# A residual block on one core: the first units' weights loaded from the middle of the output projection, and two accumulators exchanged in its second half

## The chip, the core and the metric

The kernel runs on one core of a Trainium2 chip. Its time is the device time of one execution in microseconds (us). Several executions are timed and their median is given; one more is taken with the hardware profiler, and all rows quoted below are of that one.

## What is computed

One layer on x of 512 tokens by 2048 features, all float32: a normalisation, an input projection, eight heads each of two kinds of attention, an output projection with a residual, a normalisation and a feed-forward part with 8192 hidden features.

```python
h = rmsnorm(x, g_attn);  proj = h @ w_in                  # 2048 x 6152
mixed = concat(headnorm(stick_breaking(qa, ka, va)), headnorm(forgetting(qf, kf, vf, log_f)))
x = x + mixed @ w_out                                     # 2048 x 2048: around the change
u = relu(rmsnorm(x, g_mlp) @ w_up)                        # 2048 x 8192
x = x + (u * u) @ w_down                                  # 8192 x 2048
y = rmsnorm(x, g_final)
```

## The kernel before, in words

**Numbers in two parts.** Every float32 operand is split into a high part (a rounding that ScalarE makes, a CAST of L63) and a low part (what is left, a subtraction of VectorE, L64). A product is three matmuls: high by high, high by low, low by high (L96 to L98, function mm3). ScalarE is called ACT below, VectorE DVE, TensorE PE, and SP is the engine that issues nearly all transfers. The parts of weights go into pairs of tiles named wh and wl, of which three pairs take turns.

**Seven products for eight.** The output projection, and both feed-forward matrices, are multiplied block by block in a scheme with seven products, numbered 1 to 7, of sums and differences of the four blocks of each operand. Some of the sums of w_out are made during the attention and put into DRAM (wsums, whigh). The left operand's seven forms for the output projection are G; for the feed-forward part they are F, made by left_form from hr, the new x after transposing.

**The output projection** (L682 to L762) runs through two halves of columns, db = 0 and 1, and in each through the products in the order G_ORDER = 1, 2, 6, 5, 7, 3, 4. A product has four pieces (function out_piece, m0 = 4, 6, 0, 2). For each piece SP loads a raw tile of 512 KB (wo, L630 from w_out or L632 from wsums; three raw buffers take turns), the piece is split into wh and wl, and PE runs 12 matmuls of 512 columns. Products 5 and 6 of the first half load ready high and low parts instead (L611 and L612, with wx tiles of a pool px as an additional buffer).

**The accumulators.** PSUM has three tiles A, B, C of two banks each (accoa, accob, accoc in the profile). Products 1, 6, 7 and 4 sum into A, 2 into B, 5 and 3 into C. Product 6 continues on what 1 left in A, 7 on 6, 4 on 7; 3 continues on 5. After each product take (L647) has DVE add the accumulator to a quarter of x (L651). After products 2, 7, 3 and 4 a quarter is finished: turn_quarter has PE transpose it (tr, L662), ACT copy it into hr (L665), and SP store it (xd, L666). begin (L645) loads a quarter's x ahead.

**What comes after it.** The feed-forward part's first matrix is worked off in units of 256 hidden features. A unit loads its weights in two transfers of 1 MB (L534, tiles wu of a pool rw), makes seven forms of them with DVE (L540 to L546), and runs its products in accumulators psa, psb, psc (pool ups), which stand in the same six banks as A, B and C. Later units load their weights when they are made; units 0 and 1 are loaded during the output projection. The first unit's product 1 starts when the output projection's product 4 of the second half is over.

**Who sets the order.** Each engine runs its own instructions in order. That order is written when the kernel is built: instructions go by the order of the program text, and by when their inputs and buffers come free in a simulation. issue_after(i) puts an instruction behind another on the same engine; in the loop it holds a unit's load behind the last weight transfer of the product after which it stands. A tile of a pool that takes over another pool's place waits for that tile's last reader.

**The places that the change touches** are the loop's end of a product:

```python
if db == 0 and p == 3:                      # L722: mixed is given up, rw takes its place
    mixp_cm.__exit__(None, None, None)
    rw = ctx.enter_context(tc.tile_pool(name="rw", bufs=5, side="right", reuse_waits="tile"))
if db == 1 and p in (2, 5, 7, 3):           # L725: a half of unit 0 or 1
    u, k = divmod((2, 5, 7, 3).index(p), 2)
    with tc.issue_after(ins.ins):           # ins: the product's last weight transfer
        if k == 0:
            units.append(Unit(u))
        units[u].load(k)
if db == 0 and p == 5:                      # L732: px is given up
    more_parts.pop()
    px_cm.__exit__(None, None, None)
```

and out_piece's choice of accumulator (L617), take (L647), and Unit.multiply (L554), where the first unit's three accumulators are given banks in the order c, a, b.

## Time and profile before

| what | value |
|---|---|
| median of 3 runs | 2080.78 us (2080.08 to 2081.69) |
| the profiled execution | 2079.1 us, a span of 2077.4 us |
| granted TensorE clock | 0.999 |
| busy | PE 99%, weight loads 88%, DVE 78%, ACT 51%, POOL 3% |
| moved by transfers | 394.20 MB, 190 GB/s on average |

The span is the time from the program's first instruction to its last; the execution's own time is 1.7 us longer. In a row of a timeline stand the start in us from the beginning of the span, the time taken, the engine, the line, the operation, the tile written and the tile read, and in brackets how long the engine had been idle and what ended that. A row for SP is an issue; "x4" means that four such instructions were merged, and the time is that from the first to the last one's end. A row "DMA wo<-..." is a transfer from its issue to its landing. The stretch around the output projection goes from about 630 to 810 us: its first half to 719, its second half from 720 to 804.

### The profile page before, as it was taken

The page shows a single profiled execution, that of the slowest core. Times are in us where ns is not written, and L with a number is a line of the kernel's source. Part 1 is how long each engine was busy: PE and PEld are TensorE (multiplying, and loading weights), DVE is VectorE, ACT ScalarE, POOL GpSimd, SP SyncE. Part 2 cuts the span into 40 slices and gives each one's busy share as a digit, 9 for nine tenths or more (in the row PEclk, how much of TensorE's full clock was granted, in tenths as well). Part 3 has the DMA queues.
Part 4 walks back from the last instruction along what each step waited for, and adds up shares of the span by engine and source line. Part 5 has one row for each costly group of instructions (what it writes and reads, how often), then busy time and mean ns, then how long its engine had stood idle before and what let it go on. Part 6 is the DMA issues. An engine that isn't in the chain of part 4 may idle for free.

```text
span 2077.4 us, 29812 instructions
## 1 busy us (share of the span) xinstructions
PE 2052.4 (99%) x12000; PEld 1822.5 (88%) x12000; DVE 1614.2 (78%) x1760; ACT 1049.7 (51%) x1416; POOL 54.1 (3%) x76
## 2 busy tenths in 40 slices
PE   8999999999999999999999999999999999999998
PEld 8888888888897788999999999999888888888886
DVE  6767754656579478878888888888698888989895
ACT  5434333444455456556666665666744343433434
POOL 0000000000000000000000000000000000000003
PEclk9999999999999999999999999999999999999999
DMA  7868632323236783656666566567855664764722
GB/s 233 300 233 272 220 91 74 82 80 88 75 102 217 249 271 103 221 178 191 190 206 193 189 217 189 185 201 255 288 199 225 246 234 162 289 228 147 269 96 101
DMA packets 255786, 394.20 MB, mean 190 GB/s; under 512 B 8944, under 2 KB 154400, under 8 KB 248096
## 3 DMA queue, kind: packets, MB, share of 16 engines
q1 hardware_dynamic: 254688, 390.17, 56.2%
q8 instruction: 94, 1.54, 0.3%
q10 hardware_dynamic: 960, 2.13, 0.3%
q14 instruction: 44, 0.36, 0.0%
HBM read 305.75 MB, written 86.51 MB: 189 GB/s over the span
## 4 chain that ended last, share of the span: by engine, by line
PE 92%; DVE 5%; DMA 2%; ACT 1%; issue 1%; SPq 0%; POOL 0%; ACTq 0%; DVEq 0%
PE accd L96 7%; PE accd L98 7%; PE accd L97 7%; PE psa L96 6%; PE psa L97 6%; PE psa L98 6%; PE accq L96 6%; PE accq L98 6%; PE accq L97 6%; PE psc L98 3%; PE psc L97 3%; PE psc L96 3%; PE accv L96 3%; PE accv L97 3%; PE accv L98 3%; PE psb L98 1%
## 5 line engine op out<-in xcount | busy, mean ns | idle before, releaser
L63 ACT CAST wh<-wu 128x1024 fp32r<-128x1024 f32 x171 | 178.1, 1048 | 138.5 <-PE psa L97 59.2
L64 DVE TENSOR_TENSOR wl<-wu,wh 128x1024 fp32r<-128x1024 f32 x171 | 208.1, 1221 | 48.2 <-ACT wh L63 46.9
L96 PE MATMUL psa<-f,wh 128*128 128x256 f32 x792 | 224.3, 283 | 2.3 <-ACT s L574 2.3
L97 PE MATMUL psa<-f,wh 128*128 128x256 f32 x792 | 224.1, 283 | 0.0
L98 PE MATMUL psa<-f,wl 128*128 128x256 f32 x792 | 223.9, 283 | 0.0
L63 ACT CAST wh<-wd 128x1024 fp32r<-128x1024 f32 (+1 forms) x135 | 133.3, 996 | 175.0 <-PE accd L98 105.2
L96 PE MATMUL accq<-hH,wh 128*128 128x512 f32 x512 | 200.5, 392 | 0.1
L98 PE MATMUL accq<-hH,wl 128*128 128x512 f32 x512 | 200.4, 391 | 0.0
L97 PE MATMUL accq<-hL,wh 128*128 128x512 f32 x512 | 200.3, 391 | 0.0
L63 ACT CAST wh<-wraw 128x1024 fp32r<-128x1024 f32 (+2 forms) x101 | 101.9, 1009 | 166.2 <-PE accq L97 93.6
L64 DVE TENSOR_TENSOR wl<-wd,wh 128x1024 fp32r<-128x1024 f32 (+1 forms) x135 | 153.6, 1149 | 35.4 <-ACT wh L63 34.9
L98 PE MATMUL accd<-wh,uf 128*128 128x512 f32 x432 | 168.1, 389 | 0.0
L97 PE MATMUL accd<-wl,uf 128*128 128x512 f32 x432 | 168.1, 389 | 0.0
L96 PE MATMUL accd<-wh,uf 128*128 128x512 f32 x432 | 167.9, 389 | 0.0
L64 DVE TENSOR_TENSOR wl<-wraw,wh 128x1024 fp32r<-128x1024 f32 (+2 forms) x101 | 119.4, 1183 | 60.1 <-ACT wh L63 53.8
L96 PEld LDWEIGHTS psa<-f,wh 128*128 128x128 f32 x792 | 151.9, 192 | 3.0 <-ACT s L574 2.9
L63 ACT CAST wx<-wd 128x1024 fp32r<-128x1024 f32 (+1 forms) x89 | 89.2, 1005 | 125.6 <-PE accd L98 71.8
L97 PEld LDWEIGHTS psa<-f,wh 128*128 128x128 f32 x792 | 152.0, 192 | 0.1
L98 PEld LDWEIGHTS psa<-f,wl 128*128 128x128 f32 x792 | 152.0, 192 | 0.0
L64 DVE TENSOR_TENSOR wx<-wd,wx 128x1024 fp32r<-128x1024 f32 (+1 forms) x89 | 102.6, 1160 | 24.1 <-ACT wx L63 23.9
L96 PEld LDWEIGHTS accq<-hH,wh 128*128 128x128 f32 x512 | 96.2, 188 | 19.8 <-PE accv L98 0.5
L96 PE MATMUL accd<-wx,uf 128*128 128x512 f32 x288 | 112.1, 389 | 1.1 <-ACT wx L63 1.1
(336 smaller groups left out, 5541.4 us busy)
## 6 DMA issues: line engine op xcount, KB each, us to landing
wu<-in_w_up_dram SPq DMA_DIRECT2D x64, 1024.0 KB, 6.9
ufd<-st SPq DMA_DIRECT2D x98, 512.0 KB, 7.0
wd<-in_w_down_dram SPq DMA_DIRECT2D x48, 1024.0 KB, 6.4
wraw<-in_w_in_dram SPq DMA_DIRECT2D x84, 512.0 KB, 3.9
uf<-ufd SPq DMA_DIRECT2D x42, 1024.0 KB, 6.5
mixed<-in_w_out_dram SPq DMA_DIRECT2D x8, 2048.0 KB, 8.7
wsums<-mixed SPq DMA_DIRECT2D x8, 2048.0 KB, 7.3
wo<-in_w_out_dram SPq DMA_DIRECT2D x24, 512.0 KB, 4.3
```

The lines of the kernel that those rows point to most:

```text
L63: ins = act.copy(hi, src)
L64: lows[0] = dve.tensor_tensor(lo, src, hi.bitcast(F32), op=ALU.subtract)
L96: pe.matmul(out, sh, mh, start=first, stop=False, skip_group_check=True)
L97: pe.matmul(out, sh, ml, start=False, stop=False, skip_group_check=True)
L98: return pe.matmul(out, sl, mh, start=False, stop=last, skip_group_check=True)
```

## The change

The loads of the units 0 and 1 stand at other places: before, behind products 2, 5, 7 and 3 of the second half; now, behind products 3 and 4 of the first half and 1 and 6 of the second. So that they have a place to land, mixed is given up, and rw opened, behind product 5 of the first half instead of product 3; px is given up at the same place as before. In the second half A and B are exchanged: products 1, 6, 7 and 4 sum into the pair of banks of B, and product 2 into that of A. The units' accumulators are given their banks in the order a, c, b instead of c, a, b. take has the half as an argument; its additions are the same. Size and number of all transfers, matmuls and additions stay the same.

```diff
+    FIRST_UNITS = [(0, 3), (0, 4), (1, 1), (1, 6)]
...
-                self.C, self.A, self.B = (ups.tile([P, NT], F32, tag=c, name=f"ps{c}")[:, :2 * P] for c in "cab")
+                self.A, self.C, self.B = (ups.tile([P, NT], F32, tag=c, name=f"ps{c}")[:, :2 * P] for c in "acb")
...
     A, B, C = (q.tile([P, 2, NT], F32, name=f"acco{c}") for c, q in zip("abc", (aps, bps, cps)))
+    A, B = (A, B), (B, A)
...
-        ps = {2: B, 5: C, 3: C}.get(p, A)
+        ps = {2: B[db], 5: C, 3: C}.get(p, A[db])
...
-    def take(p):
-        for q, ps in {1: [((0, 0), A)], 5: [((1, 1), C)], 6: [((0, 1), A)], 2: [((0, 0), B)], 7: [((1, 1), A)],
-                      3: [((0, 1), C)], 4: [((1, 0), A)]}[p]:
-            for t in range(2) if p == 4 else [slice(0, 2)]:
-                dve.tensor_tensor(quarter[q][:, t, :], quarter[q][:, t, :], ps[:, t, :], op=ALU.add)
+    def take(p, db):
+        q, ps = {1: ((0, 0), A[db]), 5: ((1, 1), C), 6: ((0, 1), A[db]), 2: ((0, 0), B[db]), 7: ((1, 1), A[db]),
+                 3: ((0, 1), C), 4: ((1, 0), A[db])}[p]
+        for t in range(2) if p == 4 else [slice(0, 2)]:
+            dve.tensor_tensor(quarter[q][:, t, :], quarter[q][:, t, :], ps[:, t, :], op=ALU.add)
...
-            if db == 0 and p == 3:
+            if db == 0 and p == 5:
+                more_parts.pop()
+                px_cm.__exit__(None, None, None)
                 mixp_cm.__exit__(None, None, None)
                 rw = ctx.enter_context(tc.tile_pool(name="rw", bufs=5, side="right", reuse_waits="tile"))
-            if db == 1 and p in (2, 5, 7, 3):
-
-                u, k = divmod((2, 5, 7, 3).index(p), 2)
+            if (db, p) in FIRST_UNITS:
+
+                u, k = divmod(FIRST_UNITS.index((db, p)), 2)
                 with tc.issue_after(ins.ins):
                     if k == 0:
                         units.append(Unit(u))
                     units[u].load(k)
-            if db == 0 and p == 5:
-                more_parts.pop()
-                px_cm.__exit__(None, None, None)
...
-            take(p)
+            take(p, db)
```

## The prediction

> **What bounds the kernel now.** I read the page's head first, then the table of stretches around the output projection, then the tensor engine's timeline there, and last the queue of transfers. All times below are from the profiled execution: 2079.1 us in all, a span of 2077.4.

> ```profile
> span 2077.4 us, 29812 instructions
> PE 2052.4 (99%) x12000; PEld 1822.5 (88%) x12000; DVE 1614.2 (78%) x1760; ACT 1049.7 (51%) x1416; POOL 54.1 (3%) x76
> ```

> PE is busy for all but 25.0 us. The change removes no matmul, so it can only win idle PE time, and only where it reaches: from the end of the first half of the output projection to the first units.

> ```profile
> 692.00:728.00 36.00, 35.05 (x167) 28.84 (x166) 17.36 (x17) 20.69 (x36) 0.00 (x0) 1.00 0.71 238
> 728.00:788.00 60.00, 59.60 (x272) 49.19 (x271) 43.34 (x49) 31.88 (x45) 0.00 (x0) 1.00 0.85 282
> 790.00:832.00 42.00, 39.33 (x283) 36.43 (x282) 40.85 (x50) 28.16 (x49) 0.00 (x0) 1.00 0.17 58
> ```

> Columns: stretch, length, busy PE, PEld, DVE, ACT, POOL, granted clock, share of the DMA engines, GB/s. The clock is full throughout, so it plays no part. The DMA engines are 0.71 busy in the first stretch and 0.85 in the second, which holds the four loads that the change moves. In the third DVE is the full engine: 40.85 of 42 us.

> A busy PE time hides the refill after a stall, so I count from start to start:

> ```profile
> 718.15 0.39 PE L97 MATMUL accoa<-wl,g 128*128 128x512 f32 x1
> 718.37 0.39 PE L98 MATMUL accoa<-wh,g 128*128 128x512 f32 x1
> 719.59 1.43 PE L662 MATMUL tr<-ident,x 128*128 128x128 f32 x8 [0.83 <-issue]
> 666.22 1.04 PE L662 MATMUL tr<-ident,x 128*128 128x128 f32 x8
> 759.87 0.39 PE L96 MATMUL accoc<-wh,g 128*128 128x512 f32 x1
> 760.66 0.50 PE L97 MATMUL accoc<-wl,g 128*128 128x512 f32 x1 [0.40 <-DVE wl L64]
> 791.39 0.39 PE L98 MATMUL accoa<-wh,g 128*128 128x512 f32 x1
> 791.88 0.50 PE L96 MATMUL accoa<-wh,g 128*128 128x512 f32 x1
> 793.52 0.50 PE L97 MATMUL accoa<-wl,g 128*128 128x512 f32 x1 [1.14 <-DVE wl L64]
> 823.89 0.28 PE L96 MATMUL psa<-f,wh 128*128 128x256 f32 x1
> 824.01 0.28 PE L97 MATMUL psa<-f,wh 128*128 128x256 f32 x1
> 825.60 0.39 PE L96 MATMUL psa<-f,wh 128*128 128x256 f32 x1 [1.31 <-ACT s L574]
> 833.97 0.28 PE L98 MATMUL psa<-f,wl 128*128 128x256 f32 x1
> 835.00 0.38 PE L96 MATMUL psa<-f,wh 128*128 128x256 f32 x1 [0.75 <-ACT s L574]
> ```

> An undisturbed step is 718.37 − 718.15 = 0.22 (take 0.23) for 512 columns and 0.12 for 256. Lost: at 718, 719.59 − 718.37 − 0.23 = 0.99, and 1.43 − 1.04 = 0.39 in the eight transposes; at 760, 0.56; at 791, 0.26 + 1.41 = 1.67; at 824, 1.47; at 834, 0.91. In all 5.99 us. This is the ceiling of the gain, 0.29% of the time; what a measurement of this kernel can tell from no change is about 0.2%, 4.2 us.

> **Part 1: the banks.** The last product of the first half (4) and the first of the second (1) both sum into A. So PE must wait until DVE has taken A, and the transposes of the finished quarter wait for the same. With the second half's product 1 in the other bank pair, free since product 2 of the first half, PE has twelve matmuls per piece to run while DVE takes A. No instruction is added. The gain is 0.99 + 0.39 = 1.38. It is 0 if the transposes stay first in PE's order, since they need DVE's sum whatever bank follows; below 0 it cannot go by itself. I take 1.38: the order follows what is free first, and now only the matmuls are. What comes later? The pair that product 2 of the second half takes over is emptied during product 1, a whole product ahead, and the units' banks are renamed so that unit 0 again starts in the pair that product 2 left; I cost both at nothing, covered by those phases.

> **Part 2: the four loads, where they leave.**

> ```profile
> 729.34 0.46 SPq L534 DMA_DIRECT2D wu<-in_w_up_dram  x1
> 777.22 0.46 SPq L534 DMA_DIRECT2D wu<-in_w_up_dram  x1
> 778.12 8.42 DMA wo<-wsums
> 786.63 1.05 ACT L63 CAST wh<-wo 128x1024 fp32r<-128x1024 f32 x1 [5.28 <-DMA wo<-wsums]
> 782.57 1.03 PE L662 MATMUL tr<-ident,x 128*128 128x128 f32 x8
> 787.72 1.23 DVE L64 TENSOR_TENSOR wl<-wo,wh 128x1024 fp32r<-128x1024 f32 x1 [5.10 <-ACT wh L63]
> 790.91 0.69 DVE L64 TENSOR_TENSOR f<-hr,f 128x512 fp32r<-128x512 f32 x1 [1.97 <-ACT f L63]
> 791.64 0.69 DVE L511 TENSOR_TENSOR hr<-hr 128x512 f32<-128x512 f32 x1
> 794.51 1.29 DVE L64 TENSOR_TENSOR f<-hr,f 128x512 fp32r<-128x512 f32 x2
> 795.71 2.35 DVE L64 TENSOR_TENSOR wl<-wo,wh 128x1024 fp32r<-128x1024 f32 x2
> ```

> These are the first and last of the four loads of 1 MB. The last goes out 0.9 us ahead of a weight piece of product 4, on the same queue; that piece then takes 8.42 us to land. ACT stands 5.28 us before its cast, DVE 5.10 us before the low half. That is the stall of 1.67 at 791: the matmul at 793.52 waits for a wl. Without the last two loads the pieces land early enough, and the 1.67 goes (bounds 0 and 1.67; I take all of it, since the wait of ACT is over three times as long).

> ACT runs in order, so the copies of the transposes that PE had done by 783.6 stood behind that cast too, and with them DVE's work on the left operand: 0.69 + 0.69 + 1.29 = 2.67 us that DVE did after 790 and could do before; and of the two late wl of 2.35 one, 1.18, moves ahead likewise (the other needs a buffer that PE frees last). DVE then enters its full stretch 3.85 us ahead in work, while PE enters it 1.67 earlier: 2.2 us of net relief for the waits of 824 and 834, which are 2.38 together. Part 1 shifts both engines alike. I take 2.2. The lower bound is −1.67: if DVE's chain ends no earlier, PE only arrives sooner and waits longer. The upper is 2.38. The 0.56 at 760 is again a wait for wl, with the left operand's work on DVE at the same time; I leave it, bounds 0 and 0.56.

> **Part 3: the four loads, where they arrive.** Each is issued right after the last weight piece of its product:

> ```profile
> 683.96 8.53 SPq L630 DMA_DIRECT2D wo<-in_w_out_dram  x4
> 700.28 3.03 SPq L632 DMA_DIRECT2D wo<-wsums  x2
> 709.38 5.86 SPq L630 DMA_DIRECT2D wo<-in_w_out_dram  x3
> 731.60 11.31 SPq L632 DMA_DIRECT2D wo<-wsums  x5
> q1 hardware_dynamic: 1976, 1.99, 80.3%
> ACT wh L63 <- PE accoa L98: 8.1, 5, 1.7
> ACT wh L63 <- DMA wo<-in_w_out_dram: 1.8, 1, 1.8
> wo<-in_w_out_dram SPq DMA_DIRECT2D x8, 512.0 KB, 5.1
> wo<-wsums SPq DMA_DIRECT2D x4, 512.0 KB, 3.4
> L64 DVE TENSOR_TENSOR g<-mixed,g x25: 414/685/1226, 607.9 to 674.5; 128x512 fp32r<-128x512 f32 x10, 128x256 fp32r<-128x256 f32 x8, 128x1024 fp32r<-128x1024 f32 x7
> ```

> The four SP rows hold the last pieces of products 3 and 4 (first half) and 1 and 6 (second; the fifth of the last row is product 5's first). So the loads go out near 692.5, 703.4, 715.5 and 740. The queue row is that of 829 to 837, where two such loads run with nothing else: 0.803 × 8 = 6.4 us, 3.2 us of all 16 engines for one. Three of them add 9.6 us to 692 to 728, where 0.71 × 36 = 25.6 are taken: 35.2 of 36, a share of 0.98. That is the price to fear. A load behind which SP would stand is excluded by the last row: the loads' buffers lie on mixed, whose last reader ends by 676, 16 us before the first load is due. SP's own 0.46 for an issue costs nothing: it waits for raw buffers there, as the spread of its rows shows (four issues in 8.53 us).

> What can a piece bear? PE uses one in 12 × 0.227 = 2.72 us; three raw buffers give 8.16 us a turn, less 1.05 and 1.23 for cast and low half: 5.9 us from issue to landing hold the pace. The medians of 692 to 728 are 5.1 and 3.4 (the two wo rows), and a load adds up to 3.2: 8.3 for one piece, 2.4 late. The converted tiles run two pieces ahead, 5.4 less the 2.3 that they take, about 3.1, so one late piece is covered; a second within a turn is not. In the old places four loads cost PE at most 0.56 + 1.67, a mean of 0.56, in phases where ACT and DVE also carried the left operand; in the new ones DVE is busy 17.36 of 36. I take half of 0.56 for each of the second and third load, where x and xd transfers stand beside them, nothing for the first and last, and round to 0.6. Bounds: a gain is excluded, since a load only delays; at most 3 × 3.2 = 9.6.

> [...]

> **Sum.** −1.38 − 1.67 − 2.2 + 0.6 = −4.65 us, by which the profiled 2079.1 would be 2074.4. The median of the runs is 2080.78, 1.7 above that execution; the same difference gives 2076.1.

> **The rivals.**
> *DVE is the bound behind it.* 40.85 of 42 us speak for it: the 1.67 won at 791 comes back at 824 and 834 because the sums for the units follow one another on DVE. Then Part 2 nets 0 and the sum is −1.38 + 0.6 = −0.8: 2080.0. Against it: DVE idled 5.10 and 1.97 us just before that stretch.
> *The exchange does nothing.* The transposes stay first at 718. Then −1.67 − 2.2 + 0.6 = −3.3: 2077.5.
> *The queue overflows: slower.* At 692 to 728, with the share at 0.98, the second load finds the first one's backlog. It decides from the point at which two pieces in one turn of 8.16 us take more than the 5.9 + 3.1 us. Then each load is paid in PE time up to 9.6 in all, the low halves come late to the second half too, and Part 2's 2.2 isn't won: 9.6 − 1.38 − 1.67 = +6.55: 2087.3; with two of three loads paid, +3.35. For it: the third load, x, xd and product 2's first pieces all fall within a few us after 715. Against it: in 692 to 728 ACT waits for PE 8.1 us (accoa alone) and for wo once, 1.8 us (the two rows of waits above), so raw pieces lie ready, and the load at 729.34, among the same kind of pieces, is followed by no stall in the list above.

> **How the numbers follow.** Forecast 0.48 (−4.2 to −6.0). DVE as the bound 0.17. No effect of the exchange, or a partial loss, 0.13. An overflow that two loads pay for (+3.35) or less is among the 0.13; one that all three pay for, 0.22. So faster by over 0.2% 0.48, within 0.2% 0.30, slower 0.22. The likeliest time is 2076.1; its own range 2074.8 to 2076.6. The range for 8 in 10 goes from 2074.6 (the ceiling of 5.99, and a little) to 2084.5, which leaves out half of the overflow.

> **What would show it.** Right: no gap before the transposes near 718, and matmuls of the second half ahead of them; wo landing within 5 us after 755; no cast waiting 5 us for wo near 785; the waits for L574 near 822 under 0.3 us together. Wrong: casts between 700 and 730 waiting for DMA wo and PE gaps there; gaps before psa grown beyond 2.38; SP standing before L534. It would also be wrong if stalls appear where the change does not reach, by another order of instructions.

## The result, and the profile after

The changed kernel took 2084.52 us (median of 22 runs, 2080.75 to 2087.38), the kernel before 2080.57 (22 runs): a ratio of 1.0015, 95% interval 1.0009 to 1.0021. That is 0.15% slower by this ratio and 3.95 us (0.19%) in the medians: inside the 0.2% that I had called no change, but clear of the noise of so many runs, and on the other side of the kernel before than the forecast 2076.1.

The page's head of the changed kernel; the profiled execution took 2084.65 us:

```profile
span 2082.9 us, 29807 instructions
PE 2057.6 (99%) x12000; PEld 1827.6 (88%) x12000; DVE 1613.7 (77%) x1760; ACT 1049.3 (50%) x1416; POOL 54.1 (3%) x76
```

The same work, and PE busy for 5.2 us more (2057.6 against 2052.4). So PE did not only wait longer: it also worked more slowly somewhere. The stretches of the changed kernel, with the columns as in the prediction:

```profile
692.00:728.00 36.00, 36.00 (x173) 30.05 (x172) 17.89 (x16) 17.39 (x28) 0.00 (x0) 1.00 0.90 294
728.00:788.00 60.00, 55.16 (x230) 44.16 (x229) 41.67 (x47) 32.72 (x50) 0.00 (x0) 0.94 0.69 232
790.00:832.00 42.00, 41.68 (x279) 38.28 (x278) 36.95 (x45) 28.56 (x51) 0.00 (x0) 1.00 0.19 64
```

The first and the third got better: PE is busy for all 36.00 us where 35.05 stood, and for 41.68 of 42 where 39.33 stood. The gap of 718 is gone, and so is the one of 791. The transfer engines are now 0.90 busy in the first stretch (0.71 before) and 0.69 in the second (0.85), as the move of three loads says. But in the second PE stands for 4.84 us in place of 0.40, and its granted clock is 0.94. PE's timeline there:

```profile
731.95 0.39 PE L98 MATMUL accob<-wh,g 128*128 128x512 f32 x1
733.11 0.50 PE L96 MATMUL accoa<-wh,g 128*128 128x512 f32 x1 [0.77 <-ACT wh L63]
734.37 0.50 PE L97 MATMUL accoa<-wl,g 128*128 128x512 f32 x1 [0.76 <-DVE wl L64]
735.20 0.63 PE L97 MATMUL accoa<-wl,g 128*128 128x512 f32 x1
735.63 0.63 PE L98 MATMUL accoa<-wh,g 128*128 128x512 f32 x1
741.36 0.39 PE L96 MATMUL accoa<-wh,g 128*128 128x512 f32 x1
742.67 0.50 PE L97 MATMUL accoa<-wl,g 128*128 128x512 f32 x1 [0.92 <-DVE wl L64]
765.22 0.39 PE L96 MATMUL accoc<-wh,g 128*128 128x512 f32 x1
768.00 0.50 PE L97 MATMUL accoc<-wl,g 128*128 128x512 f32 x1 [2.39 <-DVE wl L64]
```

From start to start less 0.23: 0.93 + 1.03 + 1.08 = 3.04 us lost in product 2 (accoa in the second half), and 2.55 in product 5 (accoc), where 0.56 stood before. The two rows at 735 show the second thing: the step from one matmul to the next is 735.63 − 735.20 = 0.43, not 0.23. Cut at the places where the profile's clock changes, the stretch reads:

```profile
731.69:735.10 3.41, 1.88 (x7) 1.02 (x6) 1.23 (x1) 3.09 (x8) 0.00 (x0) 1.00 0.44 170
735.10:738.51 3.41, 3.41 (x9) 2.66 (x9) 1.80 (x2) 3.41 (x8) 0.00 (x0) 0.50 0.76 217
765.82:769.23 3.41, 1.23 (x5) 1.05 (x6) 3.41 (x5) 1.04 (x1) 0.00 (x0) 1.00 0.19 18
769.23:772.64 3.41, 3.41 (x9) 2.63 (x8) 0.99 (x1) 0.56 (x1) 0.00 (x0) 0.50 0.83 292
```

Behind each of these two stalls PE runs for 3.41 us at a granted clock of 0.50: nine matmuls where fifteen fit at 0.227 a step. By estimate each such window costs about eight steps of 0.20 (0.43 − 0.23), 1.6 us.

Why the pieces come late is seen in the rows of SP, ACT and DVE around product 2 (first five) and product 5 (the rest):

```profile
719.33 1.18 SPq L535 DMA_DIRECT2D wu<-in_w_up_dram  x1
720.69 0.45 SPq L648 DMA_DIRECT2D x<-in_x_dram  x1
722.87 0.37 SPq L633 DMA_DIRECT2D wo<-in_w_out_dram  x1
724.06 0.95 SPq L669 DMA_DIRECT2D xd<-x  x1
732.01 1.04 ACT L63 CAST wh<-wo 128x1024 fp32r<-128x1024 f32 x1 [7.65 <-DMA wo<-in_w_out_dram]
747.69 0.43 SPq L535 DMA_DIRECT2D wu<-in_w_up_dram  x1
748.70 0.32 SPq L635 DMA_DIRECT2D wo<-wsums  x1
757.29 1.05 ACT L63 CAST wh<-wo 128x1024 fp32r<-128x1024 f32 x1 [3.29 <-PE accob L98]
762.80 2.00 ACT L63 CAST wh<-wo 128x1024 fp32r<-128x1024 f32 x2
763.12 1.89 DVE L64 TENSOR_TENSOR f<-hr,f 128x512 fp32r<-128x512 f32 x3
766.73 3.49 DVE L64 TENSOR_TENSOR wl<-wo,wh 128x1024 fp32r<-128x1024 f32 x3
```

(Lines have moved by up to three: L633 is L630 of before, L635 is L632, L648 is L645, L669 is L666.) The third load, x, a piece of product 2 and xd go out within 4.7 us, 2.5 MB in a row. The piece, issued at 722.87, lets ACT stand for 7.65 us and is cast at 732.01: over 9 us from issue to use. It is not alone: the piece issued at 726.33 landed after 9.3 us. In the kernel before, pieces of product 2 took 5.0 to 5.2 us; in the kernel e3_third below, where the second load stands as here and the third comes later, the two pieces whose landing the profile tells took 5.3 and 5.5. So what the second load left in the queue is small by then; it is the third with its followers that makes the pieces late. The second load has the same followers (x at 707.59, a piece at 709.79, xd at 710.92); the pieces behind it took 6.7 to 7.7 us, and PE lost nothing there. Why it delayed them less was not found.

In product 5 the delay takes a longer way. The piece behind the fourth load, issued at 748.70, took 8.5 us to land, at 757.20, and ACT stood 3.29 us ahead of its cast at 757.29. (The row names PE's last matmul as the releaser; of the three pairs that take turns, by their order the one that this cast fills had been read out nearly 4 us earlier, so I take the landing for the cause.) Everything that stands behind that cast in the order of ACT and DVE moved with it. On PE, product 6 ended at 759.8, but DVE began to add its accumulator only at 761.99; then came f three times and three more operations of the left operand. The low half that PE needed waited for all of them until 766.73, although the first of the two casts at 762.80 was done by about 763.8.

### The profile page after: what moved, and what is told of

Same layout as the page of the kernel before. It is cut to its first block, busy times and chain, and to the rows that moved or that the text cites. A ratio compares the mean times of both kernels' runs of the same rounds, so it can differ in the third digit from the quotient of the medians.

```text
span 2082.9 us, 29807 instructions
## 1 busy us (share of the span) xinstructions
PE 2057.6 (99%) x12000; PEld 1827.6 (88%) x12000; DVE 1613.7 (77%) x1760; ACT 1049.3 (50%) x1416; POOL 54.1 (3%) x76
## 4 chain that ended last, share of the span: by engine, by line
PE 92%; DVE 3%; DMA 3%; ACT 1%; issue 0%; SPq 0%; POOL 0%; ACTq 0%; DVEq 0%
PE accd L96 7%; PE accd L98 7%; PE accd L97 7%; PE psa L96 6%; PE psa L98 6%; PE psa L97 6%; PE accq L98 6%; PE accq L96 6%; PE accq L97 6%; PE psc L97 3%; PE psc L98 3%; PE psc L96 3%; PE accv L96 3%; PE accv L97 3%; PE accv L98 3%; PE psb L98 1%
## 5 line engine op out<-in xcount | busy, mean ns | idle before, releaser
L63 ACT CAST wh<-wu 128x1024 fp32r<-128x1024 f32 x171 | 178.3, 1048 | 142.1 <-PE psa L97 61.3
L64 DVE TENSOR_TENSOR wl<-wu,wh 128x1024 fp32r<-128x1024 f32 x171 | 208.1, 1222 | 48.5 <-ACT wh L63 47.4
L96 PE MATMUL psa<-f,wh 128*128 128x256 f32 x792 | 224.2, 283 | 1.0 <-ACT s L575 1.0
L98 PE MATMUL psa<-f,wl 128*128 128x256 f32 x792 | 224.2, 283 | 0.3 <-DVE wl L64 0.3
L97 PE MATMUL psa<-f,wh 128*128 128x256 f32 x792 | 224.1, 283 | 0.0
L63 ACT CAST wh<-wd 128x1024 fp32r<-128x1024 f32 (+1 forms) x135 | 133.2, 996 | 172.8 <-PE accd L98 105.0
L96 PE MATMUL accq<-hH,wh 128*128 128x512 f32 x512 | 200.5, 392 | 0.1
L98 PE MATMUL accq<-hH,wl 128*128 128x512 f32 x512 | 200.4, 391 | 0.0
L97 PE MATMUL accq<-hL,wh 128*128 128x512 f32 x512 | 200.3, 391 | 0.0
L63 ACT CAST wh<-wraw 128x1024 fp32r<-128x1024 f32 (+2 forms) x101 | 101.9, 1010 | 167.1 <-PE accq L97 93.7
L64 DVE TENSOR_TENSOR wl<-wd,wh 128x1024 fp32r<-128x1024 f32 (+1 forms) x135 | 153.6, 1149 | 34.9 <-ACT wh L63 34.4
L97 PE MATMUL accd<-wl,uf 128*128 128x512 f32 x432 | 168.1, 389 | 0.0
L98 PE MATMUL accd<-wh,uf 128*128 128x512 f32 x432 | 168.1, 389 | 0.0
L96 PE MATMUL accd<-wh,uf 128*128 128x512 f32 x432 | 167.9, 389 | 0.0
L64 DVE TENSOR_TENSOR wl<-wraw,wh 128x1024 fp32r<-128x1024 f32 (+2 forms) x101 | 119.2, 1181 | 60.5 <-ACT wh L63 54.2
L96 PEld LDWEIGHTS psa<-f,wh 128*128 128x128 f32 x792 | 151.9, 192 | 1.5 <-ACT s L575 1.4
L98 PEld LDWEIGHTS psa<-f,wl 128*128 128x128 f32 x792 | 152.0, 192 | 0.5 <-DVE wl L64 0.5
L63 ACT CAST wx<-wd 128x1024 fp32r<-128x1024 f32 (+1 forms) x89 | 89.2, 1005 | 125.3 <-PE accd L98 71.9
L97 PEld LDWEIGHTS psa<-f,wh 128*128 128x128 f32 x792 | 152.0, 192 | 0.1
L64 DVE TENSOR_TENSOR wx<-wd,wx 128x1024 fp32r<-128x1024 f32 (+1 forms) x89 | 102.6, 1160 | 24.3 <-ACT wx L63 24.1
L96 PEld LDWEIGHTS accq<-hH,wh 128*128 128x128 f32 x512 | 96.2, 188 | 19.9 <-PE accv L98 0.5
L96 PE MATMUL accd<-wx,uf 128*128 128x512 f32 x288 | 112.1, 389 | 1.1 <-ACT wx L63 1.1
## 6 DMA issues: line engine op xcount, KB each, us to landing
ufd<-st SPq DMA_DIRECT2D x98, 512.0 KB, 6.9
wraw<-in_w_in_dram SPq DMA_DIRECT2D x84, 512.0 KB, 3.9
wo<-in_w_out_dram SPq DMA_DIRECT2D x24, 512.0 KB, 3.3
```

The costliest lines, as they stand in the source:

```text
L63: ins = act.copy(hi, src)
L64: lows[0] = dve.tensor_tensor(lo, src, hi.bitcast(F32), op=ALU.subtract)
L96: pe.matmul(out, sh, mh, start=first, stop=False, skip_group_check=True)
L97: pe.matmul(out, sh, ml, start=False, stop=False, skip_group_check=True)
L98: return pe.matmul(out, sl, mh, start=False, stop=last, skip_group_check=True)
```

## The experiments

Theory 1: the loads' new places make the two stalls; the exchange of the banks is good by itself. Theory 2: the exchange makes them, since it moves the transposes, and with them xd and the next x, behind product 1's first matmuls and into the third load.

All kernels but e8_stalls and e11_loads_again, which were executed once for their profiles, were timed against the kernel before in five rounds. "Lost" is, from each one's profile, the sum over PE's matmuls between 690 and 850 us of the step from start to start less 0.227 us (512 columns), 0.119 (256) or 0.062 (128), where that is over 0.1. The part of it in steps that begin in half-speed windows stands in brackets. The column is of one execution each, and these lie off their kernels' medians by up to 4.6 us (e2_loads 4.6 and e1_banks 2.3 below, e3_third 3.1 and e10_third_split 2.5 above), so it tells where time went, and the medians what a kernel takes.

| kernel | loads behind product (first half / second half) | banks exchanged | median, us | ratio to before, 95% | lost, us |
|---|---|---|---|---|---|
| before | / 2, 5, 7, 3 | no | 2080.57 | 1 | 7.0 (0) |
| changed | 3, 4 / 1, 6 | yes | 2084.52 | 1.0015 (1.0009 to 1.0021) | 10.7 (3.1) |
| e1_banks | / 2, 5, 7, 3 | yes | 2079.01 | 0.9991 (0.9982 to 1.0000) | 4.1 (0) |
| e2_loads | 3, 4 / 1, 6 | no | 2085.18 | 1.0016 (1.0007 to 1.0025) | 8.6 (1.5) |
| e3_third | 3, 4 / 2, 6 | yes | 2080.42 | 0.9994 (0.9985 to 1.0003) | 7.8 (1.4) |
| e4_fourth | 3, 4 / 1, 5 | yes | 2081.12 | 1.0003 (0.9994 to 1.0012) | 7.5 (0) |
| e5_early | 7, 3 / 2, 5 | yes | 2078.61 | 0.9987 (0.9978 to 0.9995) | 4.4 (0) |
| e6_front | 7, 3, 4 / 2 | yes | 2078.85 | 0.9988 (0.9979 to 0.9997) | 4.7 (0) |
| e7_spread | quarters, from 4 / to 6 | yes | 2077.76 | 0.9984 (0.9976 to 0.9993) | 4.3 (0) |
| e9_spread_early | quarters, from 3 / to 2 | yes | 2076.91 | 0.9981 (0.9972 to 0.9990) | 3.5 (0) |
| e10_third_split | as changed, third in quarters | yes | 2081.21 | 1.0002 (0.9993 to 1.0011) | 8.1 (1.7) |
| e11_loads_again | as e2_loads, one execution | no | 2086.66 | | 12.4 (3.1) |
| e12_spread_old_banks | as e9_spread_early | no | 2079.34 | 0.9991 (0.9982 to 0.9999) | 4.9 (0) |

**The exchange alone.**

```diff
-    FIRST_UNITS = [(0, 3), (0, 4), (1, 1), (1, 6)]
+    FIRST_UNITS = [(1, 2), (1, 5), (1, 7), (1, 3)]
```

(and rw opened behind product 3 again.)

> The exchange of the banks alone; the four loads stand behind products 2, 5, 7 and 3 of the second half, as before. Theory 1 (the loads' new places make the two stalls at 732 to 742 and at 765): the gap of 1.4 us at the start of the second half goes, no stall is added, the stalls near 760, 791, 824 and 834 stay: about 1.4 us faster than before. Theory 2 (the exchange makes them, because the transposes, the store xd and the next x move behind product 1's first matmuls and meet the load): a new stall of about 3 us in product 2, and 2 to 3 us slower than before.

Measured: 1.8 us faster than the runs of before beside it (2080.8). PE's waits between 690 and 850:

```profile
PE psa L96 <- ACT s L575: 0.7, 1, 0.7
PE accob L97 <- DVE wl L64: 0.5, 1, 0.5
PE accoc L97 <- DVE wl L64: 0.4, 1, 0.4
PE psa L98 <- DVE wl L64: 0.3, 1, 0.3
```

No stall in product 2, none before the transposes at 718. The wait at 791 (accob now) fell from 1.1 to 0.5 without any load moved, and of the two for ACT's s near 824 and 834, 2.1 together in the kernel before, one of 0.7 is left; I had expected them to stay. Theory 2 falls in this form.

**The loads alone.**

```diff
-    A, B = (A, B), (B, A)
+    A, B = (A, A), (B, B)
```

(and the units' banks in the order c, a, b again.)

> The new places of the loads alone; A and B are not exchanged. Theory 1: both stalls (about 3 us in product 2, about 2.5 us in product 5) and a half-speed window behind each stay, and the gap of 1.4 us at the start of the second half is back: 5 to 6 us slower than before. Theory 2: the stall in product 2 is under 1 us, no half-speed window there: within 2 us of before.

Measured: 4.4 us slower, less than the 5 to 6 that I had expected, and about what the changed kernel loses with the exchange. The profile was of an execution 4.6 us below this kernel's median, so a second one was taken:

> The same kernel as e2_loads (new places, banks not exchanged), for a second profile: the first was of an execution 4.6 us below that kernel's median. If its 4.4 us over the kernel before are stalls between 690 and 850 and their half-speed windows, this profile, if it lies near the median of 2085.2, shows 11 to 12 us lost there in place of the 8.6 of the first and the 7.0 of before. If it lies near the median with no more than 9 us lost there, the cause lies elsewhere.

It took 2086.66 us and lost 12.4. Its waits of PE in the same stretch, and below them two of the kernel before:

```profile
PE tr L665 <- issue: 3.1, 1, 3.1
PE accoc L97 <- DVE wl L64: 2.6, 1, 2.6
PE psa L96 <- ACT s L575: 1.9, 2, 1.1
```

```profile
PE psa L96 <- ACT s L574: 2.1, 2, 1.3
PE tr L662 <- issue: 0.8, 1, 0.8
```

Without the exchange the late pieces show in another place: not in product 2, as theory 1 had it, but at the start of the second half. There DVE's sum, and with it the transposes, stands behind the low half of a late piece, 3.1 us in place of 0.8. It is a piece behind the second load: issued at 709.96, it landed after 7.7 us, and ACT waited 4.5 us for it. With the exchange PE has product 1's matmuls to do meanwhile. The stall in product 5 is about the same. So the loads make the loss with either banks, and the exchange decides where the first part of it is seen. The 1.9 at psa is nearly that of before (2.1): by itself the move of the loads hardly shortens it.

**The third and the fourth load, each moved alone.**

```diff
-    FIRST_UNITS = [(0, 3), (0, 4), (1, 1), (1, 6)]
+    FIRST_UNITS = [(0, 3), (0, 4), (1, 2), (1, 6)]     # e3_third
+    FIRST_UNITS = [(0, 3), (0, 4), (1, 1), (1, 5)]     # e4_fourth
```

> As the changed kernel, but the third load stands behind product 2 of the second half in place of product 1. Theory 1: the stall of 3 us at 732 to 742 and its half-speed window go, the one of product 5 stays: about 4 us less than the changed kernel, near the time of before. Theory 2: the stall in product 2 stays.

> As the changed kernel, but the fourth load stands behind product 5 of the second half in place of product 6. Theory 1: the stall of 2.6 us in product 5 falls to 0.6 or less and its half-speed window goes, the one in product 2 stays: about 3.5 us less than the changed kernel. Theory 2: no difference of over 1 us, since the exchange is the same.

Measured: 4.1 and 3.4 us less than the changed kernel. In e3_third the waits in product 2 and at the start of product 6 are 0.9 and 0.7, with no half-speed window behind them, and product 5 still stalls:

```profile
PE accoc L97 <- DVE wl L64: 2.3, 1, 2.3
PE accoa L97 <- DVE wl L64: 0.9, 1, 0.9
...
PE accob L96 <- ACT wh L63: 0.7, 1, 0.7
```

In e4_fourth it is the reverse:

```profile
PE accoa L97 <- DVE wl L64: 3.0, 3, 1.6
...
PE accoc L97 <- DVE wl L64: 0.4, 1, 0.4
```

So the fourth load makes the stall of product 5. The third makes that of product 2, but moving it does not remove all of it: from start to start e3_third still loses 1.0 us in product 2 and 0.9 at the start of product 6, whose pieces now follow the load, in place of 3.04 and a half-speed window. One more part was not as expected: in e4_fourth product 2 loses more than in the changed kernel, 4.1 us, in several stalls (the longest of the three waits above is 1.6), and none of it in steps at half speed.

**Place or amount.** Is it the load directly ahead of a piece, or the stretch's full transfer engines?

```diff
+    FIRST_UNITS = [(0, 7), (0, 3), (1, 2), (1, 5)]     # e5_early
+    FIRST_UNITS = [(0, 7), (0, 3), (0, 4), (1, 2)]     # e6_front
```

> The exchange of the banks, and the four loads behind products 7 and 3 of the first half and 2 and 5 of the second: each at least two products from the next, none behind product 1 or 6 of the second half. If a load's harm is the pieces and x, xd transfers that queue directly behind it (theory 1, by place): no stall over 1.5 us in products 2 and 5, the waits at 791 and 824 go too; 2 to 3 us faster than before (2078). If any load in the stretch of 0.7 share costs about the same (rival, by amount): 2 us slower than before.

> The exchange, and the loads behind products 7, 3 and 4 of the first half and 2 of the second. Theory 1 by place: the second and third stand in consecutive products, as in the changed kernel, but nothing follows behind product 1; a stall of under 1 us in product 1 or 2, none in product 5; 2 to 3 us faster than before. By amount: the stretch 680 to 730 carries three loads, as in the changed kernel, and 2 to 4 us slower than before.

Measured: 2.2 and 2.0 us faster than before, in line with "by place" (e6_front loses 1.4 in product 2 and 0.7 at the start of product 6, over what was expected). e6_front sends three loads ahead of 730, as the changed kernel does. The other test keeps the changed kernel's stretch and cuts the loads:

```diff
+                for c in range(0, KC // 2, 2):                      # in Unit.load, for units 0 and 1
+                    quarters.append((raw[:, c:c + 2, :], self.rows[i][:, c:c + 2, :]))
...
                 ins = out_piece(p, db, m0)
+                if quarters:
+                    with tc.issue_after(ins.ins):
+                        sp.dma_start(*quarters.pop(0))
```

> The exchange, and the same four loads in the same stretch as the changed kernel, but each in four transfers of 256 KB, one behind each weight piece from product 4 of the first half to product 6 of the second. Theory 1 as burst (a load of 1 MB makes one piece after it late): every piece is 0.8 us later instead of one by 3.2, stalls in products 2 and 5 under 1 us together, 2 to 3 us faster than before. Rival, by amount (the stretch's share of 0.98 is what hurts): stalls of 3 us and more stay, 3 to 4 us slower than before.

Measured: 3.1 us faster than before, 6.8 less than the changed kernel. Its stretch from 692 to 728, then waits (in total, times, longest): of PE from 690 to 850, and of ACT for pieces of w_out from 692 to 742.

```profile
692.00:728.00 36.00, 36.00 (x173) 30.00 (x172) 17.68 (x17) 18.19 (x30) 0.00 (x0) 1.00 0.91 309
```

```profile
PE accoc L97 <- DVE wl L64: 1.3, 1, 1.3
PE accoa L97 <- DVE wl L64: 0.9, 1, 0.9
...
ACT wh L63 <- DMA wo<-in_w_out_dram: 7.8, 3, 3.5
```

The last of these rows for the changed kernel, from 692 to 742:

```profile
ACT wh L63 <- DMA wo<-in_w_out_dram: 11.6, 2, 7.6
```

The share is 0.91 where the changed kernel had 0.90, and more bytes move (309 GB/s, 294): the amount is not less. But the longest wait of ACT is 3.5 us, not 7.6. So most of the loss comes of sending 1 MB in one transfer, with x and xd behind it, ahead of pieces that are due soon; at the places of e5_early and e6_front the same transfers in one piece cost next to nothing. The two stalls fell to 2.2 together, not to under 1 us as expected, so a part of the loss may be of the amount after all; that was not separated.

> The exchange, and the four loads in quarters of 256 KB, one behind each weight piece, as in e7_spread, but begun one product earlier: from product 3 of the first half to product 2 of the second. By burst alone the same time as e7_spread, within 1 us (2077 to 2079). If the share of the stretch counts too: the part taken out of product 6's time helps the left operand's work, stalls at 736 and 760 under 1.5 us together, and about 1 us less than e7_spread.

Begun one product earlier (the quarters' queue is filled behind product 7) it is 3.7 us faster than the runs of before beside it, 2080.63, and 0.9 less than e7_spread: the best of all these. The intervals of the two overlap, so this run does not decide whether the amount counts too.

> As the changed kernel, but the third load alone goes in four quarters, one behind each weight piece of product 2, in place of one transfer behind product 1. If the third load as one transfer makes the stall in product 2: that stall falls below 1.5 us, with no half-speed window behind it, while the stall in product 5 (fourth load) stays near 2.5 us; 2 to 4 us less than the changed kernel, about 2081. If the crowd in the queue makes it whatever the form: the stall of 3 us stays.

```diff
+            if (self.u, i) == (1, 0):
+                for c in range(0, KC // 2, 2):
+                    quarters.append((raw[:, c:c + 2, :], self.rows[i][:, c:c + 2, :]))
```

Measured: 3.3 us less than the changed kernel, and no half-speed window in product 2; but two waits of 1.9 us together remain there, above the 1.5 that I had given. From start to start product 2 still loses 0.44 + 1.82 = 2.3 us where the changed kernel lost 3.04. So the larger part of what this cut won there is the half-speed window, and this run alone does not show that the form of the load makes the stall. The quarters now stand between product 2's own pieces, which may be why; that was not tested.

> As e9_spread_early, but without the exchange of the banks: what the exchange is worth where the loads do not hurt. If it is worth the gap at the start of the second half in full: 1.4 to 1.8 us more than e9_spread_early, about 2078.5. If PE only waits elsewhere for the same: within 0.5 us of e9_spread_early.

Measured: 2.4 us more than e9_spread_early. So the exchange is worth its gap in full, and some on top: the profile without it loses 1.20 + 0.45 us around the transposes at 719 and 1.30 at 823, the one with it nothing and 0.48, against somewhat longer waits in products 2 and 5.

**The half-speed windows by themselves.**

```diff
             split(hi, lo, src[:, u0:u0 + m, :])
+            nth[0] += 1
+            if nth[0] >= 20 and nth[0] % 20 == 0:
+                for _ in range(4 + nth[0] // 20 % 4):
+                    dve.tensor_copy(lo, lo.bitcast(F32))
```

> The kernel before with artificial stalls of TensorE: in the second feed-forward matrix every twentieth low half is copied onto itself 4 to 7 times by VectorE (1.2 us each at most), ten times in all, far from any loads of units 0 and 1. If the half-speed windows come from idle time of TensorE in a window of 3.4 us: stalls of under 1.7 us leave the clock at 1, stalls of over 2.1 us bring a window of 3.41 us at 0.5 that starts on the same grid, and each such window costs about 1.6 us. If they come from transfers or from chance: no half-speed window behind these stalls.

Two long stalls of PE there and the first matmul behind a third, and stretches of 3.4 us around all three, laid by the change of the clock at 1981.20 in steps of 3.413:

```profile
1583.66 0.39 PE L98 MATMUL accd<-wx,uf 128*128 128x512 f32 x1
1587.02 0.47 PE L96 MATMUL accd<-wx,uf 128*128 128x512 f32 x1 [2.98 <-issue]
1976.78 0.39 PE L98 MATMUL accd<-wx,uf 128*128 128x512 f32 x1
1981.98 0.77 PE L96 MATMUL accd<-wx,uf 128*128 128x512 f32 x1 [4.81 <-issue]
2045.63 0.80 PE L96 MATMUL acce<-ws,us 128*128 128x512 f32 x1 [5.00 <-DVE m L986]
```

```profile
1581.90:1585.30 3.40, 2.14 (x10) 1.45 (x8) 3.40 (x3) 3.35 (x4) 0.00 (x0) 1.00 0.00 0
1585.30:1588.70 3.40, 1.68 (x7) 1.42 (x8) 3.40 (x4) 0.00 (x0) 0.00 (x0) 1.00 0.00 0
1977.80:1981.20 3.40, 0.00 (x0) 0.00 (x0) 3.40 (x5) 0.45 (x1) 0.00 (x0) 1.00 0.13 19
1981.20:1984.60 3.40, 2.62 (x6) 2.16 (x7) 3.33 (x5) 0.00 (x0) 0.00 (x0) 0.51 0.83 295
2039.30:2042.70 3.40, 1.33 (x6) 0.75 (x4) 3.40 (x4) 1.04 (x1) 0.00 (x0) 1.00 0.00 0
```

A stall of 1587.02 − 1583.66 − 0.23 = 3.13 us left the clock at 1.00, against my expectation; the line at 1585.30, 116 steps ahead of 1981.20, cuts it into 1.4 us in one window and 1.7 in the next. Behind the window from 1977.8, wholly idle, the clock was 0.51. In the one from 2039.3 PE was idle for 2.2 us, and the first matmul behind it took 0.80 us, like the 0.77 of the one at 1981.98. So half speed stood behind stalls here too, with no load of units 0 and 1 near. The length of a stall does not tell these runs apart, since 3.13 us left the clock at 1.00 here and 2.55 in the changed kernel's product 5 did not; how much of it fell into one window does (1.7 and 2.30).

## Why the prediction was wrong

**Part 1 was right.** The gap of 718 went, 1.38 as forecast; the exchange alone gained 1.8 us and, where the loads do not hurt, 2.4 (e12 to e9). The surplus is a gain that no term had: the exchange also shortens the waits at 791 and 824.

**Part 2 was right in the first term and wrong in the second.** The 1.67 of 791 went, and it goes with the loads alone (e2, e11, e12). Of the 2.38 at 824 and 834 the profile after keeps 0.48 + 0.91: 1.0 won where I took 2.2. The 0.91 stands in every profile of this study, with loads early or late, so it did not hang on DVE's backlog; I had given both waits one cause. And the 1.0 did not come from where I looked for it. With the exchange alone (e1) 0.60 is left at 824, with the move of the loads alone about 1.3 (e2, e11, e12) of 1.47. So DVE's earlier start, from which I had worked out the 2.2, was worth 0.2, and that the term had the right sign is luck. Why the exchange shortens the wait was not looked into.

**Part 3 is the step that failed**, a term of +0.6 that measured 3.04 (product 2) + 1.99 (product 5, 2.55 − 0.56) + 3.1 (two half-speed windows) = 8.1. Three things were wrong in it.

First, I let one load make one piece late, 8.3 us from issue to landing in place of the 5.9 that hold the pace, and covered that with 3.1 us of lead. But SP sends the load, x and xd in a row, with the pieces of product 2 among them: one was cast over 9 us after its issue and another landed after 9.3. That is two late pieces within one turn of the buffers, the very case that I had said was not covered. I had written the crowd into the rival ("the third load, x, xd and product 2's first pieces all fall within a few us after 715") and, with all three loads paid, given it 0.22. The rival's sum for two paying loads, +3.35, comes near the measured +3.95, but not by its mechanism: one of the two that paid is the fourth, which it did not count, and 3.1 of the loss is the clock.

Second, I costed the fourth load at nothing, looking at x and xd beside the second and third alone. That product 5 is the place where ACT and DVE carry the left operand, and where a wait of 0.56 stood already, was in my own rows. A piece that comes late there doesn't wait for itself alone: behind the cast at 757.29 DVE's addition of product 6, over by 759.8 on PE, came at 761.99, and the low half that PE needed at 766.73.

Third, the half-speed windows were in no term. "The clock is full throughout, so it plays no part" was read off a kernel whose stalls in these stretches are 1.7 us at most; nothing there showed what a longer one costs.

The sum with the measured terms is −1.38 − 1.67 − 1.0 + 8.1 = +4.1 against +3.95 in the medians. The profiled executions differ by 5.55, since the one after also has a clock of 0.50 from 629.28 to 636.11 (8.1 us lost between 600 and 690, against 6.0), behind stalls in the last attention that the kernel before has as well: 2.36 us of them fall into the 3.41 from 625.87 after, 2.04 into those from 625.95 before, where the clock stayed at 1.00.

The share of the transfer engines, which I had feared at 0.98, measured 0.90, at 294 GB/s. It was not the main cause: e7_spread moves no less in the same stretch and is 6.8 us faster than the changed kernel.

## What to carry to other kernels

Ahead of moving a prefetch "to where there is room", write down which transfers follow it on its queue and which of them is due next. Here, with the banks exchanged, four loads in quarters between the pieces cost nothing (2077.76 us, against 2079.01 with the loads at their old places), nor did they in one piece each at the places of e5_early (2078.61). In one piece each at the changed kernel's places they cost over 5 us (2084.52). Where PE is busy for 99%, count its waits from start to start and ask of each what it hangs on: one exchange of accumulators shortened three of them here. And count what a stall does to the clock: in the changed kernel 2.07 and 2.30 us of idle PE within 3.41 us were each followed by 3.41 us at a clock of 0.50, which added some 1.6 us each.

## What the runs showed of the hardware

Idle time is counted from start to start, as above, with 0.17 us for the steps of 384 columns in the attention, and cut into windows of 3.413 us by the clock's changes. In these two profiles the three windows ahead of half speed held 2.36 us of idle PE (from 625.87), 2.07 (0.93 + 1.03 + 0.11, from 731.69) and 2.30 (from 765.82). The fullest ones at full clock that were not followed by it held 2.04 us (from 625.95 in the kernel before), 1.89 (the next one there) and 1.83 (from 653.25). In e8_stalls 1.4 and 1.7 us in two windows in a row, one stall of 3.13 us, were not followed by it either, and a window without any work was. Between 2.04 and 2.07 the count, with its steps rounded to 0.01 us, is too coarse to draw a line, and why the clock halves is not shown.
